# Layer 2's output projection with the tokens on the partitions and the weights moving 512 columns at a time

## The chip, the cores and the metric

The kernel runs on one core of a Trainium2 chip. The metric is the device time of one execution in microseconds (us); several runs are made and their median is given. A profile is one further execution, recorded by the hardware profiler; its span reaches from the first to the last instruction. Engines are named as the profile names them: PE is TensorE (PEld its weight loads), DVE VectorE, ACT ScalarE, SP SyncE, whose queue SPq issues the DMAs.

## The reference

The program is a two-layer backbone over 256 latent tokens of width 2048 and 256 context tokens. In each layer a mixer is built of attention, pooling and a Fourier branch, gated, and sent through an output projection. The change touches what follows the mixer in the last layer: the projection `w_out`, the adaLN gate, the residual and the final norm, all for the 256 latent tokens.

```python
def merge_branches(att, u_pool, u_four, g, pool_w, pool_scale, fourier_w, w_out):
    mixed = jnp.concatenate([att, multiscale_pool(u_pool, pool_w, pool_scale), fourier_mix(u_four, fourier_w)], axis=-1)
    return (mixed * jax.nn.silu(g)) @ w_out
...
        x_new = x + gate[:, None] * out
...
    return rmsnorm(x, final_norm_g)
```

`out` is (256 tokens) x (2048 channels), with a contraction over 2048 mixed channels; `gate` has one value for each output channel, and `rmsnorm` divides each token by the root mean square over its 2048 channels and multiplies by `final_norm_g`.

## The kernel before

Activations lie with channels on the 128 partitions and tokens along the free axis: the residual `xs` is four tiles of 4 x 128 channels, in `[P, 4, 512]`, latent tokens in columns 0 to 255. Every large matmul is done on pairs of float32r numbers, high and low part (`split`, lines 138 to 141: ScalarE casts the high part, VectorE subtracts it to get the low part), in three products: high by high, high by low, low by high. `mm3` issues the three one after another.

Weights come in pieces of 512 KB, `[128, 1024]` float32. `wpiece` (line 143) takes a buffer `raw`, issues the DMA on SyncE's queue and splits it into `whi` and `wlo`; the pool has three buffers for each of the three names. Its instructions stand some hundred places ahead of their place in the code (`high_priority`), so loads and casts of later pieces stand in the in-order queues among earlier work.

`layer` runs one layer. In its last part, for layer 2 (`l == 1`), the mixed and gated activations of 16 contraction tiles are split into `m`, an `H` whose tiles hold high and low part side by side, 2 x 256 columns. Then the loop `for k in range(KT - nst + 1)` goes over 16 output tiles of 128 channels. Each is an `a_tile` (line 303): two weight pieces of 8 contraction tiles; for each contraction tile one matmul with `whi` stationary and both halves of `m` moving (512 columns, line 312) and one with `wlo` stationary and the high half moving (256 columns, line 313). So the output of a tile is `[128 channels, 2 x 256]` in PSUM, two halves that belong together.

`finish` adds both halves, scaled by the gate column of that output tile, to the residual (two operations of 256 columns on VectorE, line 672), squares the result on ScalarE, multiplies by the final gain there (line 677) and sums the squares on VectorE (line 682). After the last tile, `total` sums the squares over the partitions with two matmuls by ones (lines 686 and 687) and takes the root (line 691). The last lines of `backbone` (lines 952 to 961) take the reciprocal in two halves of 128 tokens, scale the 16 channel tiles in eight operations on VectorE and issue eight output DMAs of 256 KB, which write `out` as channels by tokens; the host turns it.

The tile framework sets the order on each engine from the order of the code and the priorities; waits are put in by it. `side` is a list of work that is fed between matmuls of the large loops: `side.tick` lets it issue one step.

## Time and profile before

| | |
|---|---|
| median of 3 runs | 1084.48 us |
| lowest and highest | 1084.06, 1085.44 us |
| profiled execution, its own time | 1083.26 us |
| profiled execution, span | 1081.4 us |
| mean granted TensorE clock | 0.991 of full speed |
| TensorE, VectorE, ScalarE busy | 97%, 79%, 45% of the span |

A row of the timeline gives start, duration, engine, line, operation and what it writes and reads, with the number of merged instructions behind the x; what stands in brackets is idle time of the engine before it and who ended it. Matmuls are pipelined: their records overlap, so the time that one takes from the next is the distance of their starts, not the record's length. A line of a helper stands for all its callers: 312 and 313 are `a_tile`, 336 to 338 `mm3`, 139 and 140 `split`.

### The profile page before, as it was taken

The numbers are of one execution on the slowest core, as the hardware profiler recorded it, in microseconds if no ns is written. First come the engines' busy times: TensorE is split into PE (matmuls) and PEld (weight loads), VectorE is DVE, ScalarE is ACT, GpSimd is POOL, SyncE is SP. The second block draws the span as 40 slices with busy tenths as digits, with TensorE's granted clock in tenths as the row PEclk, the third lists the DMA queues.
The fourth block names the chain that finished last, engine by engine and source line by source line (L and its number), as shares of the span: only waits on it lengthen the run. The fifth ranks groups of instructions, "written<-read, shape, count | busy, mean of one in ns | idle before, by whom it ended". The sixth has DMA issues, their size and how long they took to land.

```text
span 1081.4 us, 14324 instructions
## 1 busy us (share of the span) xinstructions
PE 1052.2 (97%) x5212; PEld 850.8 (79%) x5212; DVE 851.9 (79%) x1587; ACT 483.6 (45%) x809; POOL 0.2 (0%) x4
## 2 busy tenths in 40 slices
PE   5999999999999999999999999999999999999995
PEld 3566677888787888888888888888888888888884
DVE  6447556998999879998999887499657898878665
ACT  5223235323314675642532223288335758457551
POOL 0000000000000000000000000000000000000000
PEclk9899999999999999999999999999999999999998
DMA  9998677456685244457776557445755455765553
GB/s 358 408 342 340 230 253 252 156 197 228 211 262 169 98 137 145 158 189 268 267 285 206 195 195 260 139 149 176 264 196 185 168 199 168 260 206 181 190 184 90
DMA packets 66598, 231.56 MB, mean 214 GB/s; under 512 B 7200, under 2 KB 12384, under 8 KB 62944
## 3 DMA queue, kind: packets, MB, share of 16 engines
q1 hardware_dynamic: 66528, 230.65, 61.4%
q8 instruction: 41, 0.67, 0.3%
q14 instruction: 29, 0.24, 0.1%
HBM read 228.50 MB, written 2.11 MB: 213 GB/s over the span
## 4 chain that ended last, share of the span: by engine, by line
PE 86%; DVE 7%; issue 3%; DMA 2%; ACT 1%; SPq 0%; DVEq 0%; ACTq 0%
PE mm L338 16%; PE mm L336 16%; PE mm L337 16%; PE mm L312 10%; PE mm L828 7%; PE mm L313 5%; PE sm L828 4%; DVE ajunk L189 3%; PE sm L891 3%; PE sm L337 2%; PE sm L338 2%; PE sm L336 2%; PE sm L557 1%; DVE wlo L140 1%; DMA x<-in_xT 1%
## 5 line engine op out<-in xcount | busy, mean ns | idle before, releaser
L139 ACT CAST whi<-raw 128x1024 fp32r<-128x1024 f32 (+1 forms) x216 | 220.0, 1019 | 334.1 <-PE mm L337 111.5
L140 DVE TENSOR_TENSOR wlo<-raw,whi 128x1024 fp32r<-128x1024 f32 (+1 forms) x216 | 255.4, 1183 | 93.9 <-ACT whi L139 92.5
L189 DVE SCALAR_TENSOR_TENSOR ajunk<-araw,cbt 128x1024 bf16<-128x1024 f32 x224 | 273.9, 1223 | 47.7 <-DMA araw<-in_adar 33.7
L336 PE MATMUL mm<-whi,h 128*128 128x512 f32 x416 | 167.4, 403 | 0.0
L338 PE MATMUL mm<-whi,h 128*128 128x512 f32 x416 | 162.9, 392 | 0.0
L337 PE MATMUL mm<-wlo,h 128*128 128x512 f32 x416 | 162.9, 392 | 0.0
L336 PE MATMUL mm<-m,whi 128*128 128x512 f32 (+1 forms) x272 | 102.6, 377 | 0.0
L337 PE MATMUL mm<-m,whi 128*128 128x512 f32 (+1 forms) x272 | 102.4, 377 | 0.0
L338 PE MATMUL mm<-m,wlo 128*128 128x512 f32 (+1 forms) x272 | 102.4, 376 | 0.0
L312 PE MATMUL mm<-h,whi 128*128 128x512 f32 x256 | 92.6, 401 | 0.0
L338 PEld LDWEIGHTS mm<-whi,h 128*128 128x128 f32 x416 | 78.1, 188 | 17.0 <-DVE h L140 0.3
L336 PEld LDWEIGHTS mm<-whi,h 128*128 128x128 f32 x416 | 78.2, 188 | 15.9 <-issue 1.4
L312 PE MATMUL mm<-m,whi 128*128 128x512 f32 x256 | 90.7, 400 | 0.0
L337 PEld LDWEIGHTS mm<-wlo,h 128*128 128x128 f32 x416 | 78.2, 188 | 15.7 <-issue 1.4
L336 PE MATMUL mm<-h,whi 128*128 128x512 f32 x196 | 77.6, 396 | 0.0
L338 PE MATMUL mm<-h,wlo 128*128 128x512 f32 x196 | 76.8, 392 | 0.0
L337 PE MATMUL mm<-h,whi 128*128 128x512 f32 x196 | 76.7, 392 | 0.0
L313 PE MATMUL mm<-h,wlo 128*128 128x256 f32 x256 | 72.4, 283 | 0.0
L313 PE MATMUL mm<-m,wlo 128*128 128x256 f32 x256 | 71.7, 281 | 0.0
L828 PE MATMUL mm<-whi,h 128*128 128x512 f32 x192 | 65.3, 409 | 1.3 <-ACT h L139 1.3
L336 PEld LDWEIGHTS mm<-m,whi 128*128 128x128 f32 x272 | 51.2, 188 | 9.5
L337 PEld LDWEIGHTS mm<-m,whi 128*128 128x128 f32 x272 | 51.2, 188 | 9.4
(206 smaller groups left out, 1624.7 us busy)
## 6 DMA issues: line engine op xcount, KB each, us to landing
araw<-in_adar SPq DMA_DIRECT2D x128, 512.0 KB, 4.2
raw<-in_wb SPq DMA_DIRECT2D x78, 512.0 KB, 4.2
raw<-in_wo SPq DMA_DIRECT2D x64, 512.0 KB, 4.3
raw<-in_wg SPq DMA_DIRECT2D x55, 512.0 KB, 4.4
a<-in_ada SPq DMA_DIRECT2D x24, 1024.0 KB, 7.3
a<-in_ada SPq DMA_DIRECT2D x16, 512.0 KB, 4.6
x<-in_xT SPq DMA_DIRECT2D x4, 1024.0 KB, 6.0
cbt<-cd SPq DMA_DIRECT2D x7, 512.0 KB, 5.4
```

Source lines behind the costliest of these rows:

```text
L139: i = S.copy(hi, src)
L140: V.tensor_sub(lo, src, hi.bitcast(F32))
L189: V.scalar_tensor_tensor(junk, raw, 1.0, cbt[:, v], op0=ALU.mult, op1=ALU.mult, accum_out=acc[:, u, h, v : v + 1])
L312: PE.matmul(a.rearrange("p (s n) -> p s n", s=2), hi[:, j - j0], h.both[k][:, :, :N], start=s0, stop=False)
L313: PE.matmul(a[:, :N], lo[:, j - j0], h.hi[k][:, :N], start=False, stop=s1)
L336: PE.matmul(o, ah, bh, start=start, stop=False)
L337: PE.matmul(o, ah, bl, start=False, stop=False)
L338: PE.matmul(o, al, bh, start=False, stop=stop)
L557: PE.transpose(tp[:, h * P : h * P + P], ps[h][:, i * P : i * P + P], idt)
L828: PE.matmul(o, lt, r, start=s0, stop=s1)
L891: PE.matmul(a[32 * g : 32 * g + 32, :w_], cs[:, k], raw[:, i], start=kk == k_first, stop=kk == npc - 1, tile_position=(0, 32 * g))
```

## The change

The projection of layer 2 gets a function of its own, `out_tok`, and the loop in `layer` keeps layer 1 alone. Now tokens lie on the partitions: the stationary operand is a 128 x 128 block of `m` (one contraction tile, one of two token tiles), the moving operand 512 columns of weight. Four chunks of 512 output channels are done one after another; in chunks 0 to 2 both token tiles use a piece (two contraction tiles of 512 columns) in turn, 6 matmuls each. In the last chunk the first token tile runs three pieces (`LEAD`) ahead of the second, and pieces 0, 1, 5 and 6 take their split halves from another pool, `f4`, of four buffers.

Residual, gate and gain have to be turned as well. `turn` transposes the residual with 32 matmuls by the identity, in eight groups of four that are fed between the matmuls of chunk 0, and ScalarE copies each group from PSUM into `res`. The gate columns are transposed once, copied, written to memory as a row (`gd`) and read back onto all partitions (`grow`); the final gain comes from memory as a row (`fgr`) in two loads. `evac` multiplies a chunk by the gate row, adds the residual, squares with a running sum over the channels (`accum_out`) and multiplies by the gain; after the fourth chunk it takes the root of the sum for that token tile, scales the four chunks, two on ScalarE and two on VectorE, and issues four output DMAs of 256 KB.

```diff
+LEAD = 3
...
+        if l == 1:
+            return out_tok(xs, m, korder)
...
-                for o in (s * N - n0, N) if l == 1 else (s * N - n0,):
-                    V.scalar_tensor_tensor(x, a[:, o : o + N], gate[l][:, k, s : s + 1], x, op0=ALU.mult, op1=ALU.add)
+                V.scalar_tensor_tensor(x, a[:, s * N - n0 : s * N - n0 + N], gate[l][:, k, s : s + 1], x, op0=ALU.mult, op1=ALU.add)
...
-            if l == 1:
-                S.activation(x, x, AF.Copy, scale=fg[:, k : k + 1])
...
+    def out_tok(xs, m, korder):
+        q8, rp = late["q8"], late["rp"]
+        res = [q8.tile([P, D], F32, tag="q8", name=name("res")) for _ in range(2)]
+        grow = rp.tile([P, D], F32, tag="cbt", bufs=1, name="grow")
+        frow = [rp.tile([P, 1024], F32, tag="araw", bufs=3, name=name("frow")) for _ in range(2)]
+        for i, f in enumerate(frow):
+            nc.sync.dma_start(f, fgr[0, 1024 * i : 1024 * i + 1024].partition_broadcast(P))
+        gp = smt()
+        gc = sp.tile([P, KT], F32, tag="gcol", bufs=1, name="gcol")
+        V.tensor_copy(gc, gate[1][:, :, 0])
+        PE.transpose(gp[:KT, :P], gc, idt)
+        gr = t2("gr", (KT, P))
+        S.copy(gr, gp[:KT, :P])
+        nc.sync.dma_start(late["gd"], gr)
+        nc.sync.dma_start(grow, late["gd"].rearrange("k p -> (k p)").partition_broadcast(P))
...
+        def turn():
+            for g in range(4):
+                for tt in range(2):
+                    tp = smt()
+                    for j in range(4):
+                        PE.transpose(tp[:, j * P : j * P + P], xs[g][:, j, tt * P : tt * P + P], idt)
+                    S.copy(res[tt][:, 512 * g : 512 * g + 512], tp)
+                    yield 0.43, 1.0
+
+        side.add("turn", turn(), 2.0)
...
+        def rows(a, tt, kk, hi, lo):
+            c = slice(tt * P, tt * P + P)
+            for j in range(2):
+                k = korder[2 * kk + j]
+                mm3(a, m.hi[k][:, c], m.lo[k][:, c], hi[:, j], lo[:, j], 2 * kk + j == 0, 2 * kk + j == KT - 1)
+                side.tick(0.64)
+
+        def evac(a, ch, tt):
...
+            t = t2("og")
+            V.tensor_mul(t, a, grow[:, c])
+            V.tensor_add(x, x, t)
+            sq = t2("sq")
+            S.activation(sq, x, AF.Square, accum_out=ss[tt][:, ch : ch + 1])
+            if ch < 3:
+                V.tensor_mul(x, x, f)
+                return
+            r = sp.tile([P, 2], F32, tag="rt", name=name("rt"))
+            V.tensor_reduce(r[:, 0:1], ss[tt], axis=AX.X, op=ALU.add)
+            S.activation(r[:, 1:2], r[:, 0:1], AF.Sqrt, bias=epst, scale=1.0 / D)
+            V.reciprocal(r[:, 1:2], r[:, 1:2])
+            for q in (0, 3, 1, 2):
...
+                nc.sync.dma_start(out[tt, :, cq_], o)
+
+        for ch in range(3):
+            accs = [mmt() for _ in range(2)]
+            for kk in range(8):
+                hi, lo = wpiece(wot[ch, kk], (P, 2, 512))
+                for tt in range(2):
+                    rows(accs[tt], tt, kk, hi, lo)
...
+        for i in range(8 + LEAD):
+            if i < 8:
+                if i % 5 < 2:
...
+                        hi, lo = f4("whi", (P, 2, 512)), f4("wlo", (P, 2, 512))
+                        split(raw, hi, lo)
...
+                rows(accs[0], 0, i, *ws[i])
+            if i == 7:
+                evac(accs[0], 3, 0)
+            if i >= LEAD:
+                rows(accs[1], 1, i - LEAD, *ws[i - LEAD])
+        evac(accs[1], 3, 1)
...
-    hn = N // 2
-    tail = [slice(i * hn, i * hn + hn) for i in range(2)]
-    with tc.manual_schedule(engines={mybir.EngineType.DVE}):
-        V.reciprocal(rstd[:, tail[0]], rstd[:, tail[0]])
-        for i, c in enumerate(tail):
-            for g in range(4):
-                if i == 0 and g == TR:
-                    V.reciprocal(rstd[:, tail[1]], rstd[:, tail[1]])
-                o = xs[g][:, :, c]
-                V.tensor_mul(o, o, rstd[:, c].unsqueeze(1).to_broadcast([P, 4, hn]))
-                nc.sync.dma_start(out[:, 4 * g : 4 * g + 4, c], o)
```

The host lays `w_out` of layer 2 out as `wot` (chunk, piece, 128 rows, 2, 512), each piece contiguous as before, and needs no transpose of the result any more. Three places show the order in which instructions stand. The first is TensorE at the start of the projection; `h` are the input activations of the gate projection ahead of it, `mm` PSUM tiles. Before:

```order
L312 MATMUL mm_8599<-h_5953,whi_8624 128x512
L313 MATMUL mm_8599<-h_5953,wlo_8625 128x256
L312 MATMUL mm_8703<-m_8659,whi_8706 128x512
L313 MATMUL mm_8703<-m_8659,wlo_8707 128x256
L312 MATMUL mm_8703<-m_8660,whi_8706 128x512
L313 MATMUL mm_8703<-m_8660,wlo_8707 128x256
```

After, with `mm_8721` and `mm_8722` the two token tiles of chunk 0 and `x` the residual:

```order
L316 MATMUL mm_8600<-h_5954,wlo_8626 128x256
L729 MATMUL sm_8709<-idt,gcol 16x128
L339 MATMUL mm_8721<-whi_8725,m_8660 128x512
L340 MATMUL mm_8721<-wlo_8726,m_8660 128x512
L341 MATMUL mm_8721<-whi_8725,m_8660 128x512
...
L340 MATMUL mm_8722<-wlo_8726,m_8661 128x512
L341 MATMUL mm_8722<-whi_8725,m_8661 128x512
L742 MATMUL sm_8741<-idt,x_951_4659 128x128 x4
L339 MATMUL mm_8721<-whi_8749,m_8662 128x512
```

The pairs of 512 and 256 columns have become triples of 512, the gate's transpose stands ahead of them, and the first group of four transposes behind the twelve matmuls of the first piece.

The second place is TensorE near its end. Before, the last output tile and the sum of squares:

```order
L313 MATMUL mm_9468<-m_8656,wlo_9494 128x256
L312 MATMUL mm_9468<-m_8657,whi_9493 128x512
L313 MATMUL mm_9468<-m_8657,wlo_9494 128x256
L312 MATMUL mm_9468<-m_8658,whi_9493 128x512
L313 MATMUL mm_9468<-m_8658,wlo_9494 128x256
L686 MATMUL sm_9518<-accv_8701,ones 128x256
L687 MATMUL sm_9518<-sq_9515,ones 128x256
```

After, in the last chunk: `mm_9243` and `mm_9244` are the first and the second token tile, `whi_9247`, `whi_9259`, `whi_9283`, `whi_9301` and `whi_9319` the pieces 0, 1, 3, 4 and 5.

```order
L341 MATMUL mm_9243<-whi_9283,m_8667 128x512
L339 MATMUL mm_9244<-whi_9247,m_8660 128x512
...
L341 MATMUL mm_9244<-whi_9247,m_8661 128x512
L339 MATMUL mm_9243<-whi_9301,m_8652 128x512
...
L341 MATMUL mm_9243<-whi_9301,m_8653 128x512
L339 MATMUL mm_9244<-whi_9259,m_8662 128x512
...
L341 MATMUL mm_9244<-whi_9259,m_8663 128x512
L339 MATMUL mm_9243<-whi_9319,m_8654 128x512
```

The sum of squares has gone from TensorE. The second tile starts piece 0 when the first has ended piece 3; between its last use of piece 0 and the first tile's first use of piece 5 stand the twelve matmuls on pieces 4 and 1. Piece 5 takes piece 0's buffers.

The third place is the end of ScalarE's program. Before:

```order
L139 CAST whi_9493<-raw_9491 128x1024
L675 ACTIVATE sq_9464<-x_950_4656 128x256
L677 ACTIVATE x_950_4656<-x_950_4656,vt 128x256
L675 ACTIVATE sq_9515<-x_950_4656 128x256
L677 ACTIVATE x_950_4656<-x_950_4656,vt 128x256
L691 ACTIVATE rstd_8702<-sm_9518,epst 128x256
```

After, with `res_8702` and `res_8703` the two token tiles:

```order
L141 CAST whi_9355<-raw_9353 128x1024
L764 ACTIVATE sq_9368,ssq_8719<-res_8702 128x512
L770 ACT_TABLE_LOAD
L770 ACTIVATE rt_9370<-rt_9370,epst 128x1
L780 ACTIVATE res_8702<-res_8702,rt_9370 128x512 x2
L764 ACTIVATE sq_9409,ssq_8720<-res_8703 128x512
L770 ACTIVATE rt_9411<-rt_9411,epst 128x1
L780 ACTIVATE res_8703<-res_8703,rt_9411 128x512 x2
```

A root over a row of 256 tokens has become one of a single column for each token tile, with the load of the activation table ahead of the first, and half of the scalings now stand here.

## Rows read from the trace of the kernel before

**Rows 1.** The page's first part: engine, busy us, share of the span, instructions.

```profile
PE 1052.2 (97%) x5212; PEld 850.8 (79%) x5212; DVE 851.9 (79%) x1587; ACT 483.6 (45%) x809; POOL 0.2 (0%) x4
```

**Rows 2.** Windows: length, busy us by engine, clock, DMA share, GB/s.

```profile
976.30:1067.20 90.90, 90.90 (x515) 78.66 (x514) 60.46 (x90) 49.19 (x71) 0.00 (x0) 1.00 0.48 163
1067.20:1081.40 14.20, 1.13 (x4) 0.32 (x3) 7.62 (x12) 1.40 (x3) 0.00 (x0) 0.65 0.52 148
```

**Rows 3.** Timeline, TensorE: first pair, last 256-column matmul of the projection.

```profile
976.32 0.40 PE L312 MATMUL mm<-m,whi 128*128 128x512 f32 x1
976.55 0.28 PE L313 MATMUL mm<-m,wlo 128*128 128x256 f32 x1
...
1066.91 0.28 PE L313 MATMUL mm<-m,wlo 128*128 128x256 f32 x1
```

**Rows 4.** Timeline: the close, VectorE and SyncE's queue.

```profile
1067.23 1.00 DVE L672 SCALAR_TENSOR_TENSOR x<-mm,gate,x 128x256 f32<-128x256 f32 x2 [3.74 <-PE mm L313]
...
1069.98 0.95 DVE L954 RECIPROCAL rstd<-rstd 128x128 f32<-128x128 f32 x1 [1.75 <-ACT rstd L691]
...
1071.69 5.98 SPq L961 DMA_DIRECT2D out<-x  x8
...
1073.65 3.03 DVE L960 TENSOR_TENSOR x<-x,rstd 128x512 f32<-128x512 f32 x5
```

**Rows 5.** Timeline, TensorE: input projection of layer 2, 24 starts apart.

```profile
804.40 0.39 PE L338 MATMUL mm<-whi,h 128*128 128x512 f32 x1
...
809.84 0.39 PE L338 MATMUL mm<-whi,h 128*128 128x512 f32 x1
```

**Rows 6.** Timeline, TensorE: transposes among input-projection matmuls of layer 2.

```profile
856.39 0.27 PE L557 MATMUL sm<-idt,p 128*128 128x128 f32 x1
...
857.65 0.39 PE L338 MATMUL mm<-whi,h 128*128 128x512 f32 x1
857.88 0.60 PE L557 MATMUL sm<-idt,p 128*128 128x128 f32 x4
858.24 0.48 PE L336 MATMUL mm<-whi,h 128*128 128x512 f32 x1
858.55 0.40 PE L337 MATMUL mm<-wlo,h 128*128 128x512 f32 x1
```

**Rows 7.** Timeline: conversion of the last weight piece.

```profile
1058.63 1.05 ACT L139 CAST whi<-raw 128x1024 fp32r<-128x1024 f32 x1 [0.71 <-PE mm L312]
...
1059.71 1.23 DVE L140 TENSOR_TENSOR wlo<-raw,whi 128x1024 fp32r<-128x1024 f32 x1 [1.27 <-ACT whi L139]
```

**Rows 8.** Groups by line and shape, layer 2: busy us, mean ns, idle before.

```profile
L672 DVE SCALAR_TENSOR_TENSOR x<-mm,gate,x 128x256 f32<-128x256 f32 x32 | 15.5, 484 | 12.8 <-PE mm L313 12.3
...
L140 DVE TENSOR_TENSOR ptl<-sm,pth 128x512 fp32r<-128x512 f32 x16 | 10.8, 686 | 1.6 <-PE sm L337 1.3 <-ACT pth L139 0.3
...
L544 DVE RECIPROCAL nm<-nm 128x1 f32<-128x1 f32 x16 | 2.4, 158 | 0.5 <-ACT p L540 0.5
...
L545 ACT ACTIVATE p<-p,nm 128x512 f32<-128x512 f32 x16 | 11.3, 725 | 1.2 <-DVE nm L544 1.2
...
L467 ACT ACTIVATE sq<-raw 128x512 f32<-128x512 f32 x4 | 2.4, 624 | 0.0
...
L540 ACT ACTIVATION_READ_ACCUMULATOR p<-sm,nm,ny 128x1 f32 x16 | 3.1, 196 | 0.0
```

**Rows 9.** DMA issues: count, KB each, us to landing; last row: the outputs.

```profile
x<-in_xT SPq DMA_DIRECT2D x4, 1024.0 KB, 6.0
...
cd<-crow SPq DMA_DIRECT2D x1, 16.0 KB, 4.3
...
DMA to landing us min/median/max: 2.4/2.9/3.6
```

**Rows 10.** Timeline, ScalarE: a table load and the root behind it.

```profile
990.14 1.28 ACT L680 ACT_TABLE_LOAD   x1
991.43 0.20 ACT L680 ACTIVATE dum<-sq 128x1 f32<-128x1 f32 x1
```

More of the change, by code (lines that the diff above doesn't have):

```diff
@@ L67, in backbone @@
     wo: bass.AP,
+    wot: bass.AP,
+    fgr: bass.AP,
     wgs: bass.AP,
@@ L163, in load_cb @@
         late["cd"] = cd.rearrange("(v k) p -> v (k p)", v=2)
+        late["gd"] = dp.tile([KT, P], F32, name="gd")
     def ada_units():
@@ L687, in total @@
                     PE.matmul(ss, ones, sq, start=False, stop=True)
-                    if l == 0:
-                        rstd_row(ss, rstd[:, n0:n1])
-                    else:
-                        S.activation(rstd, ss, AF.Sqrt, bias=epst, scale=1.0 / D)
+                    rstd_row(ss, rstd[:, n0:n1])
                 return total
         for k in range(KT - nst + 1):
-            total = finish(k, a_tile(wo[l, k], m, korder, nt, FILL[l][4]), range(nst))
-            if l == 0 and k == 10:
+            total = finish(k, a_tile(wo[k], m, korder, nt, FILL[l][4]), range(nst))
@@ L697, in layer @@
+            if k == 10:
                 pool_tables(1)
                 rope_tables(1)
-        if l == 1:
-            total()
-        if l == 0:
-            k = KT - 1
-            ws = [wpiece(wo[l, k, half], (P, 8, P)) for half in range(2)]
-            for s in range(2):
-                a = mmt()
-                c = slice(s * N, s * N + N)
-                for half, (hi, lo) in enumerate(ws):
-                    for j in range(8):
-                        kk = korder[half * 8 + j]
-                        mm3(a[:, :N], hi[:, j], lo[:, j], m.hi[kk][:, c], m.lo[kk][:, c], half + j == 0, half * 8 + j == 15)
-                        if s == 1 and half == 0 and j == TJ:
-                            late["between"](xs, rstd, total)
-                total = finish(k, a, (s,))
-            def later():
-                yield 0.0, 3.0
-                total()
-                yield 0.4, 0.0
-            side.add("ss", later(), 0.0)
@@ L721, in layer @@
-        return xs, rstd
+        k = KT - 1
+        ws = [wpiece(wo[k, half], (P, 8, P)) for half in range(2)]
+        for s in range(2):
+            a = mmt()
+            c = slice(s * N, s * N + N)
+            for half, (hi, lo) in enumerate(ws):
+                for j in range(8):
+                    kk = korder[half * 8 + j]
+                    mm3(a[:, :N], hi[:, j], lo[:, j], m.hi[kk][:, c], m.lo[kk][:, c], half + j == 0, half * 8 + j == 15)
+                    if s == 1 and half == 0 and j == TJ:
+                        late["between"](xs, rstd, total)
+            total = finish(k, a, (s,))
@@ L949, in backbone @@
     late["make_ctx"] = make_ctx
-    xs, rstd = layer(1, h1, xs, lambda: (b_chunk(1, 0, h1, 2, 0), {}, None, None))
-    hn = N // 2
-    tail = [slice(i * hn, i * hn + hn) for i in range(2)]
-    with tc.manual_schedule(engines={mybir.EngineType.DVE}):
-        V.reciprocal(rstd[:, tail[0]], rstd[:, tail[0]])
-        for i, c in enumerate(tail):
-            for g in range(4):
-                if i == 0 and g == TR:
-                    V.reciprocal(rstd[:, tail[1]], rstd[:, tail[1]])
-                o = xs[g][:, :, c]
-                V.tensor_mul(o, o, rstd[:, c].unsqueeze(1).to_broadcast([P, 4, hn]))
-                nc.sync.dma_start(out[:, 4 * g : 4 * g + 4, c], o)
+    layer(1, h1, xs, lambda: (b_chunk(1, 0, h1, 2, 0), {}, None, None))
 def _order():
@@ L1033, in _layout @@
     wo = np.concatenate([w_out[:, 1024:], w_out[:, :1024]], 1)
-    t["wo"] = wo.reshape(2, 2, 8, P, KT, P).transpose(0, 4, 1, 3, 2, 5)
+    t["wo"] = wo[0].reshape(2, 8, P, KT, P).transpose(3, 0, 2, 1, 4)
+    t["wot"] = wo[1].reshape(8, 2, P, 4, 512).transpose(3, 0, 2, 1, 4)
+    t["fgr"] = final_norm_g.reshape(1, D)
     def sw(g):
@@ L1044, in _layout @@
     return {n: np.ascontiguousarray(a) for n, a in t.items()}
-_NAMES = ["xT", "vec", "cb", "ada0", "adar", "wb", "wg", "wo", "wgs", "gqk", "pw", "fw", "rope", "band", "icnt", "dft0", "cc", "sel", "ident"]
+_NAMES = ["xT", "vec", "cb", "ada0", "adar", "wb", "wg", "wo", "wot", "fgr", "wgs", "gqk", "pw", "fw", "rope", "band", "icnt", "dft0", "cc", "sel", "ident"]
 def _result(y):
-    return np.ascontiguousarray(y.transpose(2, 1, 0)[np.argsort(_order())]).reshape(1, N, D)
+    return np.ascontiguousarray(y.reshape(N, D)[np.argsort(_order())]).reshape(1, N, D)
 def kernel(**inputs):
@@ L1061 @@
         args[n] = nc.dram_tensor(f"in_{n}", a.shape, mybir.dt.from_np(a.dtype), kind="ExternalInput").ap()
-    args["out"] = nc.dram_tensor("out_0", (P, KT, N), F32, kind="ExternalOutput").ap()
+    args["out"] = nc.dram_tensor("out_0", (2, P, D), F32, kind="ExternalOutput").ap()
     with tile.TileContext(nc) as tc:
```

31 lines of the change are left out of this document (30 added, 1 removed).

## The prediction

> **What bounds the kernel now.** I read the page's first part, then the stage that changes, then the prices of what replaces it. TensorE is busy for 97% of the span [rows 1], so the work of another engine counts only where TensorE waits for it or has ended. [...] The stage holds 256 pairs: a 512-column matmul and a 256-column one, 0.35 us from one pair to the next; the first starts at 976.32, the last 256-column one at 1066.91 [rows 3], and with its own 0.12 the columns end at 1067.03.
>
> Behind it comes a **closing chain** with no matmul of weight in it: the records end at 1067.19, the last two gate-and-add operations start at 1067.23, the reciprocal of the row norms at 1069.98, then eight scalings on VectorE until 1076.68, their eight output DMAs issued until 1077.67, and the program's end at 1081.4 [rows 4]. That is 14.2 us [rows 2], of which 3.7 lie behind the last issue.
>
> So there are two questions: does TensorE leave the projection earlier or later, and how long is the close.
>
> **TensorE's columns.** Before: 256 x (512 + 256) = 196,608 columns. After: 2 token tiles x 4 chunks x 16 contraction tiles x 3 = 384 matmuls of 512, the same 196,608. The gain can only come from the number of instructions, 512 to 384. The new form (activations stationary, 512 weight columns moving) already runs in layer 2's input projection: from 804.40 to 809.84 there are 24 starts, 0.2267 us each [rows 5]. 384 x 0.2267 = 87.05. Beside transposes a start comes 0.23 after the one ahead of it (857.65 to 857.88, [rows 6]); were it 0.23 for all, 88.3. I take the first value, since three of the four chunks have no side work, and keep 88.3 as the bound. Against 1067.03 - 976.32 = 90.7 that saves 3.7 (2.4).
>
> **The transposes** are new on TensorE: 8 groups of four for the residual and one of the gate columns. A group of four costs, from the matmul start before it (857.65) to the second start behind it (858.55), 0.90 less two ordinary 0.2267, so 0.45 [rows 6]. 8 x 0.45 + 0.1 = 3.7. They eat the saving exactly: TensorE should leave the projection near 1067.1, as before (bounds: 1066.7, if the short waits of the first tile go, to 1068.5).
> What the row shows is 0.11 to 0.12 per transpose. [...]
>
> **Weights.** There are 32 pieces of 512 KB as before; each needs a ScalarE cast and a VectorE difference, 1058.63 to 1060.94 = 2.31 from start to finish [rows 7]. A piece now lasts 12 x 0.2267 = 2.72 on TensorE (before 2.83). In chunks 0 to 2 the three buffers leave the conversion two pieces' time, 5.4, so it stays hidden. In the last chunk the first tile runs three pieces ahead; two extra buffers make five. The order shows that the cast of piece 5 waits for the second tile's last use of piece 0, and 12 matmuls stand between that and the first use of piece 5: 2.72 plus one matmul until its low half is read, against 2.31 plus the waits' ends. That leaves some 0.4 us each for pieces 5, 6 and 7. I cost it at nothing; the cover is thin, and each us beyond it is a us.
>
> **Evacuations and rows.** VectorE loses the 32 gate-and-add operations of 0.48, 15.5, and gains 22 operations of 512 columns at 0.69, 15.2 [rows 8]: off the path in both. The ones at a chunk's end stand in the queue ahead of later weight differences; behind the first of them is the third piece of the next chunk, due 5.4 later, and the six take 4.1. ScalarE's eight copies in chunk 0, each near the 0.62 of its 512-column square [rows 8], lie between casts that have three pieces of lead. The gate row goes through memory: ScalarE's copy is behind the cast of piece 3 (about 980.5), the write takes up to 4.3, the broadcast of 1 MB about the 6.0 of another 1 MB load [rows 9]; landing near 991, and first needed at 976.4 + 90 x 0.2267 + 3.6 = 1000.4. On SyncE the broadcast waits for the write, and behind it is the load of piece 7, whose buffer is free only near 985 anyway. The two broadcasts of the final gain come 50 us early. All of this is costed at nothing, covered by 9 us or more. Layer 1 keeps its order.
>
> **The close, second token tile**, from TensorE's end T. First multiply at T + 0.04 (as now), 0.69; add 0.69; then ScalarE's square 0.62 with its accumulator read, some 0.75; sum, square root 0.20 and reciprocal 0.16 on single columns, with hand-overs of 0.04, some 0.6 [rows 8, 10]. The scale stands at T + 2.9. Two scalings on ScalarE (0.73) and two on VectorE (0.69) run side by side until T + 4.3; the first output is issued at T + 3.65. Four issues at 0.4 to 0.75 each (eight took 5.98 [rows 4], there paced by VectorE) end at T + 5.25 to 6.65; behind the last one I take the 3.7 of now. End: T + 9.0 (9.0 to 10.3; with the quickest landing, 2.4 [rows 9], instead of one near 3.6, T + 7.9). 14.2 becomes 9.0: **5.2 us less**.
>
> **The first token tile** closes while TensorE works on: its last matmul is 24 x 0.2267 = 5.44 before T. Its chain: 2.2 to the end of the square, table load 1.29 [rows 10], root and reciprocal 0.45, scalings 1.4: 5.35. VectorE is free for the second tile at about T - 0.1, just in time.
> In the row the activation behind the load starts 1.29 after the load's start. [...]
>
> **Sum** on the profiled execution: span 1081.4, its own time 1083.26. Columns -3.7, transposes +3.7, close -5.2: span 1076.2, time 1078.1. The runs' median, 1084.48, lies 1.2 above the profiled time; the same difference gives **1079.3**, 0.48% less.
>
> **Rivals.**
> [...]
> 2. No change: transposes at the 0.27 of their own record [rows 6], 32 x 0.27 = 8.6 instead of 3.6, eat the close's gain: 1084.3. Against: four start within 0.36 here. Partial waits of the same size at the chunk borders end here too.
> 3. Slower: the weight conversion falls behind. Place: pieces 2 and 3 behind each chunk's evacuation and pieces 5 to 7 of the last chunk, nine in all, because in-order VectorE and ScalarE hold evacuations ahead of them. Price: a piece that is late by its whole conversion stops TensorE for 2.31. Four such (9.2) outweigh the 5.2 and the margin: 1088.5; all nine, 1100. Against: VectorE and ScalarE would be busy for about 60 of 91 us. It decides from the fourth late piece on.
> That the change does not do what it says is settled by the order: 384 matmuls and 33 transposes stand there.
>
> **How the numbers follow.** A run of this kernel can't tell less than about 0.2% from no change: 1082.3 to 1086.6 counts as the same. Forecast 0.74, own range 1077.4 (close T + 7.9, short waits gone) to 1082.0 (88.3 for the columns, T + 10.3); rival 1 0.06, rival 2 0.12, rival 3 0.08. Faster 0.80, same 0.12, slower 0.08. The range runs from 1077.4 to 1082.8: both bounds of the forecast, rival 1, and waits of some 0.8 on top of the dearer columns and close; that holds 0.8.
>
> **What the changed profile would show.** TensorE's new matmuls 0.227 apart in chunks 1 to 3 and no idle time in chunk 3; the transposes' groups 0.36 long; the last matmul near 1067; one table load between the two closes; four outputs issued 3.7 after the end of the matmuls; the program's end 9 us behind them. A gap of TensorE before the pieces 5 to 7 or at a chunk's start, or a wait of the first multiply for the gate row, would make the prediction wrong; so would a close in which the second tile's multiply finds VectorE busy.

## The result, and the profile after

The changed kernel takes 1079.78 us (median of 4 runs, 1078.94 to 1080.07); the kernel before, run beside it, 1084.96 (4 runs, 1084.06 to 1086.55). The ratio is 0.995 with a 95% interval of 0.9937 to 0.9962: faster, by about 5 us. Forecast were 1079.3 and a range of 1077.4 to 1082.8. Run once more in a later series it gave 1080.19 against 1084.81, ratio 0.9958 (0.9945 to 0.9971). The profiled execution took 1079.74, its span is 1078.0.

The page's first part answers [rows 1]: engine, busy us, share of the span, instructions.

```profile
PE 1051.0 (98%) x5113; PEld 846.1 (78%) x5113; DVE 842.6 (78%) x1562; ACT 481.6 (45%) x807; POOL 0.2 (0%) x4
```

The windows answer [rows 2]: the projection from its first matmul to TensorE's end, then the close. Columns: stretch, length, busy us of each engine, granted clock, DMA share, GB/s.

```profile
977.65:1069.12 91.47, 91.47 (x419) 75.13 (x416) 55.65 (x70) 45.97 (x66) 0.00 (x0) 1.00 0.52 173
1069.12:1078.00 8.88, 0.00 (x0) 0.00 (x0) 2.85 (x6) 2.35 (x5) 0.00 (x0) 0.74 0.62 236
```

TensorE is idle nowhere in the projection, as before; the projection is no shorter (91.5 against 90.9 us), and the close went from 14.2 to 8.9. On TensorE's timeline, the first matmul, the first group of transposes with its neighbours, and the last matmul (they answer [rows 3, 6]; columns: start us, us, engine, line, operation, shapes, count):

```profile
977.65 0.47 PE L339 MATMUL mm<-whi,m 128*128 128x512 f32 x1
...
980.27 0.40 PE L341 MATMUL mm<-whi,m 128*128 128x512 f32 x1
980.51 0.60 PE L742 MATMUL sm<-idt,x 128*128 128x128 f32 x4
980.86 0.48 PE L339 MATMUL mm<-whi,m 128*128 128x512 f32 x1
981.18 0.40 PE L340 MATMUL mm<-wlo,m 128*128 128x512 f32 x1
...
1068.73 0.39 PE L341 MATMUL mm<-whi,m 128*128 128x512 f32 x1
```

A group costs 981.18 - 980.27 = 0.91 less two ordinary starts of 0.2267: 0.45, as [rows 6] had it. The close on the timelines of VectorE, ScalarE and SyncE's queue (it answers [rows 4, 10]):

```profile
1065.82 1.28 ACT L770 ACT_TABLE_LOAD   x1
...
1068.31 0.48 DVE L778 TENSOR_SCALAR res<-res,rt 128x512 f32<-128x512 f32 x1
1069.16 0.69 DVE L761 TENSOR_TENSOR og<-mm,grow 128x512 f32<-128x512 f32 x1 [0.36 <-PE mm L341]
1069.88 0.69 DVE L762 TENSOR_TENSOR res<-res,og 128x512 f32<-128x512 f32 x1
...
1072.08 0.75 DVE L776 SCALAR_TENSOR_TENSOR res<-res,rt,frow 128x512 f32<-128x512 f32 x1
...
1068.40 6.23 SPq L781 DMA_DIRECT2D out<-res  x8
```

The last scaling of the first token tile (1068.31) ends just ahead of the second tile's first product (1069.16), which waits for TensorE and not for VectorE; the bracket gives the idle time between them, 0.36 us. The eight outputs are issued from 1068.40 to 1074.63. Those of the first tile move from 1069.2 to 1072.1, behind TensorE's end but while the second tile's close is still computing. What no row of the page tells at once is what the end then waits for. One window of the kernel before, in the middle of its output, shows DMA engines that are full (share 1.01) at 294 GB/s:

```profile
1074.00:1075.00 1.00, 0.00 (x0) 0.00 (x0) 1.00 (x3) 0.00 (x0) 0.00 (x0) 0.50 1.01 294
```

and one of the kernel after, also full, at 385:

```profile
1075.00:1076.00 1.00, 0.00 (x0) 0.00 (x0) 0.00 (x0) 0.00 (x0) 0.00 (x0) 0.50 1.01 385
```

So both closes end shortly behind the last bytes of the output: before, 2.1 MB move from 1072.6 to 1080.1, and the end comes 1.3 later; after, the second tile's 1.05 MB alone move from 1073.7 to 1076.5, and the end comes 1.4 later.

### The profile page after: what moved, and what is told of

It is laid out like the page before. It is cut to its first block, busy times and chain, and to the rows that moved or that the text cites. A ratio compares the mean times of both kernels' runs of the same rounds, so it can differ in the third digit from the quotient of the medians.

```text
span 1078.0 us, 14095 instructions
## 1 busy us (share of the span) xinstructions
PE 1051.0 (98%) x5113; PEld 846.1 (78%) x5113; DVE 842.6 (78%) x1562; ACT 481.6 (45%) x807; POOL 0.2 (0%) x4
## 4 chain that ended last, share of the span: by engine, by line
PE 66%; DVE 6%; issue 3%; DMA 2%; ACT 0%; ACTq 0%; SPq 0%; DVEq 0%
PE mm L339 16%; PE mm L340 16%; PE mm L341 16%; PE mm L315 5%; PE mm L316 3%; DVE ajunk L192 3%; PE sm L340 2%; PE sm L339 2%; PE sm L341 2%; PE sm L560 2%; DVE wlo L142 1%; DMA cbt<-cd 1%; PE sm L523 1%; DMA araw<-in_adar 0%; DVE ss L471 0%
## 5 line engine op out<-in xcount | busy, mean ns | idle before, releaser
L341 PEld LDWEIGHTS mm<-m,wlo 128*128 128x128 f32 x272 | 51.2, 188 | 9.4
L315 PEld LDWEIGHTS mm<-h,whi 128*128 128x128 f32 x256 | 48.1, 188 | 10.9
```

The source lines that it names most:

```text
L315: PE.matmul(a.rearrange("p (s n) -> p s n", s=2), hi[:, j - j0], h.both[k][:, :, :N], start=s0, stop=False)
L341: PE.matmul(o, al, bh, start=False, stop=stop)
```

## The experiments

Each kernel differs from the changed one by the edit shown; `...` in a diff stands for lines left out. Stage lengths are read from the traces; where a median is given, it stands beside the kernel before's in the same series.

**Without the lead (lead0).** Does the second tile's close need the first one out of the way?

```diff
-LEAD = 3
+LEAD = 0
```

> LEAD is 0 in place of 3: in the last chunk the two token tiles take each weight piece one after the other, so that the first tile ends 6 matmuls (1.36 us) before the second and not 24 (5.44 us). The theory: the first tile's close, with its table load of 1.28 us, then lies in the way of the second's on VectorE and ScalarE. Laid out with the durations of the changed kernel's trace, the second tile's scalings start some 5.1 us after the last matmul and not 2.96, and the span is 2.2 us longer (1.9 to 2.6), all of it behind the last matmul: 8.9 us become 11.1. The projection itself stays at 91.3 us. A first rival: the two closes run side by side and the lead is worth nothing (span +0.3 at most). A second: each close waits for the whole of the one before (+3.8). Of the pace inside the last chunk: the pieces from the f4 buffers still take 0.2333 us a matmul and the others 0.2267, if it is the place of the buffer that sets it; if the interleaving of the two tiles sets it, the 0.2333 is gone.

Measured: 1082.73 us against 1084.36, ratio 0.9988 (0.9976 to 1.0). The projection is 91.1 us from first to last start, as with the lead; TensorE's end comes at 1069.58, the program's 11.4 behind it and not 8.8: +2.5, within the theory's 1.9 to 2.6, but not by its mechanism alone. Timeline of VectorE's second scaling and of SyncE's queue, and one window:

```profile
1074.29 0.75 DVE L776 SCALAR_TENSOR_TENSOR res<-res,rt,frow 128x512 f32<-128x512 f32 x1
...
1073.05 4.46 SPq L781 DMA_DIRECT2D out<-res  x8
...
1078.00:1079.00 1.00, 0.00 (x0) 0.00 (x0) 0.00 (x0) 0.00 (x0) 0.00 (x0) 0.50 1.01 385
```

The scaling is 4.7 behind TensorE's end, only 1.75 later than with the lead. What sets the end is transfer: all eight outputs are issued from 1073.05 on, the first 3.5 behind TensorE's end (with the lead the second tile's first output is issued 3.7 behind it), and 2.1 MB move from 1073.9 to 1079.5 with full DMA engines, 5.6 us in place of 2.9. The lead is worth 2.5 us because half of the output is out before the other half is ready. In the last chunk the f4 pieces kept 0.2333 a matmul: it is not the interleaving.

**One piece further ahead (lead4).** Is the conversion's cover gone with four?

```diff
-LEAD = 3
+LEAD = 4
```

> LEAD is 4: five pieces of the last chunk are held at once, as many as there are buffers, so that pieces 5, 6 and 7 can be converted only when TensorE has let go of the piece before and wants the new one at once. The theory that the cover of three pieces ahead is thin but there: TensorE now stands three times for a conversion of 2.3 us, and the projection is 7.2 us longer (6.5 to 8.0), the close as before; the clock may add to it where the stalls let it fall. The rival, that the conversion runs well ahead of TensorE in any case: no stall, and the span within 0.5 us of the changed kernel's 1078.0.

Measured: a miss of the theory. One run, 1080.09; projection 91.5 us, at a granted clock of 1.00 throughout, no wait of a piece's length. The scheduler doesn't keep the order of the code: it sets matmuls of the second tile between those that would wait. Order of TensorE's instructions (line, destination tile, weight and activation tile; `mm_9243` is the first token tile, `whi_9313` the sixth piece):

```
L340 MATMUL mm_9244<-wlo_9260,m_8663 128x512
L339 MATMUL mm_9243<-whi_9313,m_8654 128x512
L341 MATMUL mm_9244<-whi_9259,m_8663 128x512
L339 MATMUL mm_9244<-whi_9271,m_8664 128x512
L340 MATMUL mm_9244<-wlo_9272,m_8664 128x512
L341 MATMUL mm_9244<-whi_9271,m_8664 128x512
L340 MATMUL mm_9243<-wlo_9314,m_8654 128x512
```

What is left is 0.4 us in the last chunk, two starts 0.1 late among it; as much again falls in the close. Timeline of VectorE:

```profile
1069.13 0.48 DVE L778 TENSOR_SCALAR res<-res,rt 128x512 f32<-128x512 f32 x1
1069.52 0.68 DVE L761 TENSOR_TENSOR og<-mm,grow 128x512 f32<-128x512 f32 x1
```

TensorE ends at 1069.05; the product starts 0.47 behind that and not 0.04, with no idle time ahead of it, because the filled-in matmuls let the first tile end later. The close is longer by the same 0.43.

**Without the transposes (no_turn).**

```diff
+        one = sp.tile([P, 1], F32, tag="one", bufs=1, name="one")
+        V.tensor_scalar(one, gc[:, 0:1], 0.0, 1.0, op0=ALU.mult, op1=ALU.add)
...
-                    tp = smt()
-                    for j in range(4):
-                        PE.transpose(tp[:, j * P : j * P + P], xs[g][:, j, tt * P : tt * P + P], idt)
-                    S.copy(res[tt][:, 512 * g : 512 * g + 512], tp)
+                    o = res[tt][:, 512 * g : 512 * g + 512].rearrange("p (j n) -> p j n", j=4)
+                    S.activation(o, xs[g][:, :, tt * P : tt * P + P], AF.Copy, scale=one)
```

> The 32 transposes of the residual are left out; ScalarE copies the residual from SBUF untransposed in the same eight pieces (so that the residual is not turned). The theory, eight groups at 0.45 us each on TensorE's stream: the projection goes from 91.3 to 87.6 us (-3.6, 3.3 to 3.9), and the span by as much. The first rival, by the transposes' own records of 0.27 us each: -8.6 us. The second, transposes hidden beside the matmuls: 0. Five of the eight copies run ahead of the last gate evacuations on ScalarE, which may shift the projection's start by some tenths; the projection's own length is what decides.

Measured: 1076.8 against 1084.36, ratio 0.9931 (0.9909 to 0.9954). First and last matmul of the projection:

```profile
980.74 0.48 PE L339 MATMUL mm<-whi,m 128*128 128x512 f32 x1
...
1068.13 0.39 PE L341 MATMUL mm<-whi,m 128*128 128x512 f32 x1
```

87.4 us between them, 91.1 with transposes: 3.7 for 32, the theory's 0.45 a group. One costs 3.7 / 32 = 0.115 us of TensorE's stream, and not the 0.27 of a record that stands alone. Of the 3.1 us by which the projection starts later than in the changed kernel, 2.8 were there by 320 us into the program, far ahead of the edit.

**Half as wide (halves).** Is it the width of the moving operand that pays?

```diff
-                mm3(a, m.hi[k][:, c], m.lo[k][:, c], hi[:, j], lo[:, j], 2 * kk + j == 0, 2 * kk + j == KT - 1)
+                for o in (slice(0, 256), slice(256, 512)):
+                    first = 2 * kk + j == 0 and o.start == 0
+                    last = 2 * kk + j == KT - 1 and o.start == 256
+                    mm3(a[:, o], m.hi[k][:, c], m.lo[k][:, c], hi[:, j, o], lo[:, j, o], first, last)
```

> Each 512-column matmul of the layer 2 output projection is two of 256 columns into the two halves of the same accumulator, with the same weights: twice the matmuls and the weight loads, the same columns. The theory, 256 columns at 0.1181 us as in the kernel before: 384 x (0.2362 - 0.2267) = +3.6 us on the projection (91.3 to 94.9; 3.0 to 4.0), the close unchanged. The rival, that the wider moving operand gave nothing and the gain lies in the close alone: within 0.5 us of 91.3. Of the f4 pieces: if the place of the operand costs 0.0066 us a matmul of 512 columns, they are again slower than the others, by some 0.003 us for each half.

Measured: 1084.45 against 1084.36, ratio 0.9994 (0.9979 to 1.0008): of the gain nothing is left. The projection is 95.4 us from first to last start, +4.3, above the range of 3.0 to 4.0. Two starts ten apart in the second chunk:

```profile
1019.80 0.28 PE L341 MATMUL mm<-whi,m 128*128 128x256 f32 x1
...
1021.00 0.28 PE L339 MATMUL mm<-whi,m 128*128 128x256 f32 x1
```

0.1200 each. With 0.2267 for 512 columns that makes (0.2267 - 0.1200) / 256 = 0.417 ns a column and 0.0133 us beside the columns for a matmul of either width, an estimate from these two paces. In chunks 1 and 2 the 96 added matmuls cost 1.28 each time, 96 x 0.0133; chunk 0 with its transposes and chunk 3 with its f4 pieces paid 0.9 each. The expectation had taken 0.1181 for 256 columns and was too low for that. Its last part failed: from f4 buffers the halves were to be slower, and they are a little quicker. In the last chunk 24 matmuls of the second token tile, all from f4 buffers, take 2.85 us, 0.1188 each:

```profile
1069.84 0.28 PE L339 MATMUL mm<-whi,m 128*128 128x256 f32 x1
...
1072.69 0.28 PE L339 MATMUL mm<-whi,m 128*128 128x256 f32 x1
```

**The table load (table_early, table_twice).** Two runs belong together: the load taken out of the first tile's close, and a second one put in.

```diff
+                if ch == 2 and tt == 1:
+                    d2 = sp.tile([P, 1], F32, tag="dum", name=name("dum"))
+                    S.activation(d2, ss[1][:, 2:3], AF.Sqrt)
```

> ScalarE computes one more Sqrt, of a number that exists only after the third chunk, so that the table load of 1.28 us moves from the first token tile's close to the middle of the projection. The theory that the first tile's close was just out of the way (VectorE idle for 0.36 us ahead of the second tile's first product): the close of the second tile stays at 8.9 us after the last matmul (8.7 to 9.0), and only that idle time grows, to 1.6 us. The rival, the table load on the path to the end: 7.6 to 7.9 us.

This execution is of no use: it took 3728.99 us, with 0.84 us from one 512-column matmul to the next through the whole program, at a granted clock of 1.00; why isn't known. The second kernel has that early Sqrt too, and in the close a Tanh:

```diff
+            if tt == 0:
+                d3 = sp.tile([P, 1], F32, tag="dum", name=name("dum"))
+                S.activation(d3, ss[0][:, 3:4], AF.Tanh)
```

> Beside the Sqrt after the third chunk ScalarE computes a Tanh of one column in the first token tile's close, just ahead of its square root, so that two table loads of 1.28 us stand in that close and not one. Laid out with the trace's durations, the first tile's reciprocal ends 1.6 us later, at 0.1 us after the last matmul; the second tile's product goes ahead of the first tile's scalings on VectorE, and its addition waits for them: 1.27 us later than in the changed kernel. The theory, the slack of 0.36 us used up: the end 10.1 us after the last matmul in place of 8.9 (9.8 to 10.4). The rival, that the first tile's close isn't in the way at all: 8.9.

Measured: 1081.91 in one run, the close 9.8 us and not 8.8 (+0.9; expected +1.2, at the edge of the range). ScalarE's two loads, and VectorE's addition, which now waits for the first tile's scalings:

```profile
1067.03 1.28 ACT L775 ACT_TABLE_LOAD   x1
...
1068.54 1.28 ACT L776 ACT_TABLE_LOAD   x1
1069.84 0.29 ACT L776 ACTIVATE rt<-rt,epst 128x1 f32<-128x1 f32 x1
...
1072.03 0.69 DVE L762 TENSOR_TENSOR res<-res,og 128x512 f32<-128x512 f32 x1
```

From one load's start to the next are 1.51 us: the load's 1.28, the Tanh's 0.20 and 0.03 more. And the early load did what the lead of four did not: it stands on ScalarE ahead of the sixth piece's cast. On TensorE's timeline the low half is late:

```profile
1056.89 0.66 PE L339 MATMUL mm<-whi,m 128*128 128x512 f32 x2
1058.08 0.50 PE L340 MATMUL mm<-wlo,m 128*128 128x512 f32 x1 [0.53 <-DVE wlo L142]
```

The last chunk is 0.85 us longer. The cover of the conversion there is thinner than one table load.

**The table load at a harmless place (table_moved).**

```diff
-        dum = sp.tile([P, 1], F32, tag="dum", name=name("dum"))
-        S.activation(dum, epst, AF.Sqrt)
...
                 side.finish("turn")
+                dum = sp.tile([P, 1], F32, tag="dum", name=name("dum"))
+                S.activation(dum, res[1][:, D - 1 : D], AF.Square)
+                S.activation(dum, dum, AF.Sqrt)
```

> The early Sqrt reads the last column of the turned residual, so that its table load of 1.28 us runs on ScalarE after the last group of transposes, ahead of the evacuation of the first chunk, and no longer in the first token tile's close; this takes the place of the run in which it stood after the third chunk and in the way of the sixth piece's conversion. The theory that the load was hidden in the changed kernel by 0.36 us: the end stays 8.84 us behind the last matmul (8.7 to 9.0), VectorE's idle time ahead of the second tile's product grows from 0.36 to between 1.3 and 1.7 us, and the projection stays at 91.1 us, since the conversion there has more than two pieces of cover. The rival, the load on the path to the end: 7.6 to 7.9 us. A second rival, the load stalls a piece here too: the projection 0.5 us longer or more.

Measured: the projection 91.1 us, the close 8.83: unchanged. (The run's 1078.24 is an early start, 976.15.) VectorE's product of the second tile:

```profile
1067.65 0.69 DVE L759 TENSOR_TENSOR og<-mm,grow 128x512 f32<-128x512 f32 x1 [1.45 <-PE mm L341]
```

Only its idle time grew, from 0.36 to 1.45. The load was hidden in the changed kernel, by a third of a microsecond.

The two lines that the diff takes out are an early root of the changed kernel itself, which could have loaded the table ahead of the close. It reads a constant and waits for nothing, so it stands in layer 1, behind another root that has just loaded the table:

```profile
561.16 0.19 ACT L735 ACTIVATE dum<-epst 128x1 f32<-128x1 f32 x1
```

At 848.78 another function's table was loaded (line 543), and the close had to load that of the root once more. The moved root reads a result, and stands where it was put, at 994.58.

**The f4 buffers moved (f4_shift).** The last chunk of the changed kernel takes 21.89 us, although a chunk without transposes takes 96 x 0.2267 = 21.76 and one start less is counted in the last.

```diff
+    pad = sp.tile([P, 96], F32, tag="pad", bufs=1, name="pad")
+    nc.vector.memset(pad, 0.0)
```

> A filler of 384 bytes a partition stands ahead of the f4 buffers, so that they have the same offset as the other weight buffers within every 16 KB; the buffers that lie above move up with them, the instructions and their order are the same. Four of the eight pieces of the last chunk lie in f4 buffers, and their matmuls took 0.2333 us and not 0.2267. The theory, the offset of the moving operand sets this: all at 0.2267, the last chunk from 21.89 to 21.55 us, the span -0.3. The rival, that it is the region of the memory (above 168 KB a partition) or the pool as such: 0.2333 again and 21.89. Where earlier stages read f4 buffers (the attention's keys and values), their pace may change too, in either direction; by the last matmul ahead of the projection that is told apart from the projection itself.

Measured: 1078.37 against 1084.3, ratio 0.9941 (0.9924 to 0.9959); the last chunk 21.53 us, all starts 0.2267 apart. Pieces 5 and 6 of the second tile, 12 matmuls from f4 buffers; first the changed kernel,

```profile
1064.79 0.40 PE L339 MATMUL mm<-whi,m 128*128 128x512 f32 x1
...
1067.58 0.39 PE L339 MATMUL mm<-whi,m 128*128 128x512 f32 x1
```

then the one with the filler:

```profile
1064.07 0.39 PE L341 MATMUL mm<-whi,m 128*128 128x512 f32 x1
...
1066.79 0.39 PE L341 MATMUL mm<-whi,m 128*128 128x512 f32 x1
```

2.79 us become 2.72. The pace follows the place: a shift of 384 bytes settles it, in the same region and pool. What of the place counts was not taken apart further.

**Output in 512-byte pieces (packets512).**

```diff
-                nc.sync.dma_start(out[tt, :, cq_], o)
+                nc.sync.dma_start(out[tt, 4 * q : 4 * q + 4].rearrange("j p n -> p j n"), o.rearrange("p (j n) -> p j n", j=4))
...
```

Left out are the shape of the output and the host's reading of it.

> The output is laid out in blocks of 128 columns, so that each output transfer moves 512 bytes in one piece and not 2048, as the kernel before did; bytes, issues and everything else are as in the changed kernel. The theory: the end waits for the second token tile's 1.05 MB, at 286 KB a microsecond with pieces of 512 bytes (the rate of the kernel before's output) and at 385 with pieces of 2048: 3.67 us and not 2.72, so that the end lies 9.85 us behind the last matmul and not 8.9 (9.6 to 10.1). The rival, the end set by the issues and a fixed landing time: 8.9.

Measured: 1080.36 against 1084.3, ratio 0.9962 (0.9947 to 0.9977); the close 9.70 us against 8.84: +0.86. The window in the middle of the second tile's output:

```profile
1075.00:1076.00 1.00, 0.00 (x0) 0.00 (x0) 0.00 (x0) 0.00 (x0) 0.00 (x0) 0.50 0.98 284
```

The DMA engines are about as full as with 2048 bytes (share 0.98 against 1.01), and move 284 GB/s and not 385: a quarter less.

**Both kernels once more (before_again, after_again).** No edit; the question is what two executions differ by.

> The kernel before, once more with a profile: the projection began at 976.32 us in its first profile and at 977.65 in that of the changed kernel, whose instructions up to there are the same; in the five later profiles with these instructions ahead it began between 977.2 and 978.1. The theory, that this is the difference of two executions: the start lies anywhere between 976.0 and 979.0 and the first 320 us carry most of it. The rival, that the change delays the work ahead of the projection (buffers and inputs lie elsewhere): 976.3 again, to within 0.3. The stage itself: 90.7 us for the projection in either case.

Measured: 1082.12, span 1080.2. First and last matmul of the projection, and between them two wide starts, one pair apart, on TensorE's timeline:

```profile
976.78 0.40 PE L312 MATMUL mm<-m,whi 128*128 128x512 f32 x1
...
1029.85 0.39 PE L312 MATMUL mm<-m,whi 128*128 128x512 f32 x1
...
1030.20 0.39 PE L312 MATMUL mm<-m,whi 128*128 128x512 f32 x1
...
1065.79 0.28 PE L313 MATMUL mm<-m,wlo 128*128 128x256 f32 x1
```

The start is 0.46 later than in the first profile, against 0.3 at most in the rival. In eleven profiles of the changed kernel and its variants (table_early's left aside), with TensorE's same instructions ahead, it lies between 975.76 and 980.74: scatter, as the theory had it, though not all in the first 320 us, and wider. It arises where nothing was changed: of the changed kernel's new instructions ahead of the projection the early root (see table_moved) stands at 561 and the others behind 948, and TensorE takes 90.67 us from its 2600th matmul to its 3000th (550 to 641 us) and 52.3 from its 4400th (924) to the projection in all thirteen profiles, with differences of 0.03 at most. That buffers and inputs lie elsewhere is not excluded by this. The close, 14.2 us behind the projection's last record, is as before. But the projection, which neither theory had in doubt, takes 89.0 us from first to last start and not 90.6. Sixteen pairs take 5.547 us through most of it, 0.3467 a pair; in the first profile 5.65, 0.3531 a pair, with the same instructions, buffers and granted clock (1.00). The wide matmul makes the difference, 0.230 against 0.236. The gate projection just ahead has pairs of the same shapes; there sixteen pairs take 5.65 us in all thirteen profiles (table_early's left aside), the slower pace. From the changed kernel's:

```profile
950.77 0.40 PE L315 MATMUL mm<-h,whi 128*128 128x512 f32 x1
...
956.42 0.40 PE L315 MATMUL mm<-h,whi 128*128 128x512 f32 x1
```

> The changed kernel once more, beside the two kernels before it in this list and the next: a ratio of 0.995 (0.9935 to 0.9965), a projection of 91.1 us and an end 8.84 us behind the last matmul; the projection starts between 976.5 and 979.

Measured: ratio 0.9958 as told above; start 977.09, projection 91.08 us from first to last start, close 8.84, each as in the first profile of it. From the first matmul of the projection to the end both executions take 100.3 us; the kernel before takes 105.1 and 103.5.

**A shorter end (half_end).** The filler, the moved table load, the quicker scaling first, and the last two pieces of the second tile in two halves, the upper one into an accumulator of its own; the diff shows the last of these, without the changes of `evac`:

```diff
...
-            if i >= LEAD:
+            if LEAD <= i < LEAD + 6:
                 rows(accs[1], 1, i - LEAD, *ws[i - LEAD])
-        evac(accs[1], 3, 1)
+        b = mmt()
+        for h, o in enumerate((slice(0, 256), slice(256, 512))):
+            for kk in range(6, 8):
+                hi, lo = ws[kk]
+                for j in range(2):
+                    k = korder[2 * kk + j]
+                    mm3((accs[1], b)[h][:, :256], m.hi[k][:, P:], m.lo[k][:, P:], hi[:, j, o], lo[:, j, o], h == 1 and 2 * kk + j == 12, 2 * kk + j == KT - 1)
+        evac(accs[1], 3, 1, b)
```

> Built from what the runs showed: the 384-byte filler of the f4 buffers (last chunk -0.36 us); the table load moved as in table_moved; for the second token tile the last two pieces of the last chunk go as 256-column matmuls, first all those of the lower half, then those of the upper half into an accumulator of their own (12 x (2 x 0.1200 - 0.2267) = +0.16 us), so that VectorE adds what is there while TensorE still works and only 256 columns are left to multiply, add and square after the last matmul; and VectorE's shorter scaling (0.48 us and not ScalarE's 0.65) feeds the first output. The theory: the last matmul 0.20 us earlier against the projection's start, the end 7.9 us behind it and not 8.84 (7.6 to 8.2), 1.1 us in all; the median near 1078.6 if the changed kernel's is 1079.8. The rival, VectorE still busy with the first tile's close when the lower half is there: 8.3 to 8.8.

Measured: 1077.82 (6 runs) against 1084.81, ratio 0.9935 (0.9919 to 0.9951), beside 1080.19 of the changed kernel in the same series. TensorE ends at 1067.04. VectorE's part behind that:

```profile
1067.08 0.42 DVE L769 TENSOR_TENSOR og<-mm,grow 128x256 f32<-128x256 f32 x1
1067.54 0.42 DVE L770 TENSOR_TENSOR res<-res,og 128x256 f32<-128x256 f32 x1
...
1069.26 0.49 DVE L785 TENSOR_SCALAR res<-res,rt 128x512 f32<-128x512 f32 x1
```

The scale stands 2.2 us behind TensorE's end and not 2.96, the close is 7.87 us; from the projection's first matmul to the end 99.15 us and not 100.3: 1.16 less, of 1.1 expected. The medians lie 2.4 apart; between the two profiled executions what exceeds 1.16 is an earlier start of the projection (975.76 against 977.09), and it is not claimed. It beats both kernels on the stage that it changes.

## Why the prediction was right, step by step

- **What bounds the kernel.** Right: TensorE is never idle in the projection of either kernel (busy 90.90 of 90.90 us before and 91.47 of 91.47 after, at a granted clock of 1.00), so the stage is its own pace, and the gain had to come from that or from the close.
- **TensorE's columns.** The mechanism was right, the size was off, for two reasons. The new matmuls do run 0.2267 apart in chunks 1 and 2; in the last chunk the f4 pieces take 0.2333, 48 x 0.0066 = 0.3 us, which f4_shift removes (0.35 off the last chunk). And the 90.7 us that were to be beaten belong to one execution: in the other, the same kernel before took 89.1. Without transposes the projection is 87.6 us with its last matmul's own 0.23, so the columns save 3.1 or 1.5 and not 3.7.
- **The transposes.** Right: 3.7 forecast, 3.7 measured by no_turn. They took more than the columns gave.
- **TensorE's end.** 91.3 us behind the projection's start were measured, 90.7 forecast: 0.6 too few, within the bound of 88.3 for the columns. 0.35 of it are the f4 pieces, 0.2 stand in the first chunk (25.67 us, where 21.76 and 3.7 were to be expected).
- **Weights.** Costed at nothing, and rightly: no gap ahead of pieces 5 to 7. That the cover is thin was right too: a table load ahead of one cast cost 0.85 in table_twice. That a lead of four would use it up, as was expected of lead4, was wrong, since the scheduler fills the gap.
- **Evacuations and gate row.** Right: the broadcast issued at 983.8 landed 5.5 later, at 989.3; the first product that reads it starts at 1003.0.
- **The close.** T + 9.0 forecast, T + 8.84 measured; the scale at T + 2.9 forecast, 2.96 measured, the first output issued at T + 3.65 forecast, 3.71 measured. But the prediction took the 3.7 us behind the last issue as a landing time, and so the end as set by the issues. The traces show transfers that fill the DMA engines: 2.1 MB at about 286 GB/s before, 1.05 MB at 385 after. That the end came out right is partly luck: the last issue ended at T + 5.5 and not T + 5.25, and the end came 3.3 behind it and not 3.7. By the rates some 0.7 MB were then still to move in either close. In the traces the bytes that the end waits for start 5.4 us behind the projection's last record before and 4.5 after, and move for 7.5 and 2.9 us. Of these 4.6 us the half that leaves early is 3.7 (in packets512, with the old pieces, the second tile's half moves for 3.8), the longer pieces 0.9 (packets512: 0.86). With the longer pieces, losing the early half costs 2.5 (lead0).
- **The first token tile's close.** VectorE was to be free at T - 0.1 and was at T - 0.33. Just in time, as said: table_moved gains nothing, lead4 and table_twice push it over the edge and pay.
- **The sum.** Span 1076.2 forecast, 1078.0 measured: 1.3 from a later start of the projection (977.65 against 976.32), 0.6 from the projection, -0.1 from the close. The later start arises ahead of 924 us, where TensorE has the same instructions in both kernels: between executions it lies anywhere from 975.76 to 980.74 in eleven profiles of the changed kernel and its variants, and in the kernel before at 976.32 and 976.78. The median, 1079.78, is 0.5 above the forecast. That the medians lie 5.2 apart, just the sum forecast, is partly luck: from the projection's first matmul to the end the gain is 4.8 against one execution of the kernel before and 3.2 against the other.
- **The range.** Three of its bounds don't follow from their terms: with the quickest landing 9.0 - 1.2 is T + 7.8, not 7.9; a close of T + 7.9 and TensorE's end at 1066.7 give 1077.8, not 1077.4; and 88.3 for the columns gives TensorE's end at 1068.3, not 1068.5. The time measured lies inside either way.

Of the rivals, the first stands in the range and in the chances with a second 1.29 us at the one switch of tables, which no run shows: in the changed kernel the root starts 1.30 behind the load's start (1065.82 to 1067.12), and a second load, put into that close, made it 0.9 longer (table_twice). Transposes at 0.27 each fell with no_turn. Late pieces did not occur.

Open is how much of the 5 us between the medians is the stage: 4.8 against one execution of the kernel before, 3.2 against the other. Which pace of its projection is the common one isn't known, since two profiles of it are all there are; that the gate projection kept the slower one in all thirteen speaks for 4.8, but doesn't show it.

## What to carry to other kernels

At a program's end ask what the last transfers weigh. Here half of the output leaves while the other half is still being computed, and in pieces of 2 KB; the close gained 5.4 us, while on TensorE the transposes took back what the columns gave, and more (3.7 against 3.1 or 1.5). Before a saving is worked out from one trace, look whether the stage keeps its pace from one execution to the next: the projection before took 90.6 us in one and 89.0 in the other. A side job of one microsecond on an engine that converts weights belongs where the buffers are furthest ahead, which here was right behind a stretch in which TensorE had other work (a load of 1.28 us cost the projection nothing there, in table_moved, and 0.85 ahead of the sixth piece's cast, in table_twice). And a root that is to load a table early needs an input that holds it at its place: the one that reads a constant stood at 561 us, the one that reads a result at 994.58.

## What the runs showed of the hardware

- The pace of these float32r matmuls depends on where the moving operand lies: in the last chunk 0.2333 us for 512 columns in the f4 buffers, 0.2267 in the others, and 0.2267 in both when the f4 buffers lie 384 bytes further (f4_shift, half_end). With 256 columns the f4 buffers were not the slower ones: 0.1188 against 0.1200 (halves).
- In chunks 1 and 2, outside the f4 buffers, a matmul took 0.2267 us with 512 columns and 0.1200 with 256 (halves). By an estimate from these two, 0.0133 us of either is not in the columns.
- Alternating 512- and 256-column matmuls ran at 0.3531 us a pair in one execution and 0.3467 in another, through the whole stage and at the same granted clock; in the gate projection ahead of it 0.3531 in all thirteen profiles. The second value is 0.2267 and 0.1200, the paces of the two widths in chunks 1 and 2; what made the first was not found.
- Output in pieces of 512 bytes moved at 279 to 294 GB/s with full DMA engines (share 1.01 to 1.03), in pieces of 2048 at 385 (share 1.01).
